# Gram matrices stored by row, inverse inputs in 2 loads, one PSUM bank moved from the chain's output to the passes

## The chip, the core and the metric

The kernel runs on one core of a Trainium2 chip. What is measured is the device time of one execution, in microseconds (us); smaller is better. The core has a matrix engine (PE), three engines for elementwise work (DVE, ACT, POOL), and an engine SP that here does nothing but issue nearly all DMAs. Every engine works through its own list of instructions in a fixed order, so an instruction that waits holds up all that stand behind it on the same engine. PE's results go to PSUM, which this kernel uses as 8 banks of 128 partitions x 512 fp32.

## What is computed

One block of a hybrid network, for 2048 tokens of width 1024, in fp32. A normalised input is multiplied by one wide weight matrix; two branches use the result, and their gated outputs are added to the input:

```
h = rms_norm(x, norm_g) * (1 + scale) + shift
p = h @ w_in                       # 1024 x 5960, in parts: pr pk pv pwd pad z_a q ckv z_b qi ki wi g_a g_b
y_a = rwkv7_branch(pr, pk, pv, pwd, pad, ...)      # a recurrence over all tokens, 8 heads of 64
    # per token: state = state*w + (state a) b^T + v k^T ; y = state r
y_b = dsa_branch(q, ckv, qi, ki, wi, ...)          # attention over the 256 best keys of each query
merged = sigmoid(g_a) * ((y_a * silu(z_a)) @ w_pa) + sigmoid(g_b) * ((y_b * silu(z_b)) @ w_pb)
out = rms_norm(x + gate * (merged @ w_o), final_g)
```

Only the recurrence (`rwkv7_branch`) is touched by the change.

## The kernel before

Each fp32 operand of a large product is split into a high and a low part, and a product is the sum of three matmuls (high x high, high x low, low x high). Tokens are cut into 4 blocks of 512. The stages, in the time of the trace: the start up to 130 us, the index GEMM up to 400, the selection of keys up to 840; from there to 1740 the recurrence, with the rest of the wide GEMM laid between its steps; the first branch's product (`branch_a`) from 1699 to 1816, attention up to 2240, the finish up to 2534.

The wide GEMM is done in units (`unit`, L251): 48 matmuls `g`, of 24 k-steps and two halves of 256 columns, into one of two banks named `g`, which ACT or DVE then empties into an SBUF tile `eo` (`evacuate`) for a store. Its last jobs make the gates: columns `g`, stored to `gg` in DRAM.

The recurrence of one block of 512 tokens has three parts.

- `rwkv_pass` (L612 to L720), per pair of heads: loads rows of the wide product (`pk`, `pr`, `pv`), makes decays and keys, and the Gram matrices of 64-token chunks: `pg` at L703, masked by DVE into `gt` (L705) and stored to `gmd` in DRAM (L706). Its PSUM tiles are all named `pg` and come from the pool `rwpa` (L544).
- `rwkv_inv` (L722 to L747): loads `ln` from `gmd` (L730), 64 problems (8 chunks x 8 heads) for each diagonal 32 x 32 sub-block, and inverts them on DVE by 31 steps of forward substitution (`prd` L740, `tm` L742), then stores the inverses.
- `rwkv_chain` (L749 to L821): 8 chunks one after the other, each of which needs the state `H` of the chunk before. A chunk loads its matrices (`gmc` at L762 among them), then PE does `zu`, `pp`, `zu`, `hp` (L777 to L801), and DVE forms the new state from `hp` (L806). Every four chunks `chain_norm` and `chain_out` normalise the outputs `y`; PE transposes them into a tile `co` (L854), DVE scales them (L855), and a store sends them to `ya`. The tiles `zu`, `pp`, `hp` and `co` are one PSUM bank each.

The 8 banks of this stage are thus 2 for `g`, 4 for the chain and 2 for `pg`; after the last pass `heads` (L862) takes the two of `pg` for its own products `p`.

The order on each engine is set ahead of time by a scheduler: each part of the program has a priority (`self.band`, L1246 to L1286: pass 50000, chain 50000 to 55000, GEMM 60000 to 70000, `branch_a` 75000), and the scheduler places instructions by a simulated timeline in which a tile's buffer must be free. A larger number is later work that fills in. DMAs stand in SP's list in the same way; each one also waits for the DMA eight places before it in its lane of eight semaphores.

Where the GEMM ends, `branch_a` starts. It first splits its weights `w_pa`, in four chunks of 128 x 1024, into `w_pah` and `w_pal` (L1018 to L1020), in SBUF space that the GEMM's pools leave, and so only when the last `gg` store has landed; then its `br` matmuls (L1111) run, whose inputs `uh` and `ul` come from `z` and `y` (L1042 to L1051), and `y` from `ya`.

Of the kernel before, what the change touches and what calls it, by code (L numbers as in the profile page):

```python
# [24 lines left out]
FT = mybir.dt.float32  # L25
# [6 lines left out]
PSUM = bass.MemoryType.PSUM  # L32
# [5 lines left out]
NTB = S // TB  # L38
# [13 lines left out]
class Block:  # L52
# [479 lines left out]
    def rwkv_open(self, ctx):  # L532
        nc, x = self.nc, self.x
        V, A, G, DMA = nc.vector, nc.scalar, nc.gpsimd, nc.sync
        R = self.R = {}
        c1 = R["c1"] = self.pool("rwc", 1, side="right", ctx=ctx)
        R["ch"] = self.pool("rwch", 2, side="right", ctx=ctx)
        R["pctx"], R["qctx"], R["ictx"] = ExitStack(), ExitStack(), ExitStack()
        R["iv"] = self.pool("rwi", 1, side="right", ctx=R["ictx"])
        R["ld"] = self.pool("rwl", 2, side="right", ctx=R["pctx"])  # L540
        R["wk"] = self.pool("rww", 1, side="right", ctx=R["pctx"])
        R["st"] = self.pool("rws", 2, side="right", ctx=R["pctx"])
        R["pc"] = self.pool("rwpc", 1, PSUM, ctx=R["qctx"])
        R["ps"] = self.pool("rwpa", 2, PSUM, ctx=R["pctx"])  # L544

        def cols(n):
            R[n] = self.cols(c1, x[n], "c_" + n, 4)

        for n in ("w0", "a0", "k_k", "k_a", "r_k", "lnx_g", "lnx_b"):
            cols(n)  # L550
        for n, src in (("w0h", "w0"), ("a0h", "a0"), ("kah", "k_a")):
            R[n] = c1.tile([128, 4], FT, name=n)
            V.tensor_scalar(R[n], R[src], 0.5, None, op0=OP.mult)
        R["kai"] = c1.tile([128, 4], FT, name="kai")
        V.tensor_scalar(R["kai"], R["k_a"], -0.5, 1.0, op0=OP.mult, op1=OP.add)

        wa2 = R["ld"].tile([128, 512], FT, name="pk")
        DMA.dma_start(wa2[0:64], x["w2"])
        DMA.dma_start(wa2[64:128], x["a2"])
        w2, a2, l2 = (c1.tile([128, 512], FR, name=n) for n in ("w2s", "a2s", "wa2l"))  # L560
        R["w2"], R["a2"], R["l2"] = w2, a2, l2
        A.copy(w2[0:64], wa2[0:64])
        A.copy(w2[64:128], wa2[0:64])
        A.copy(a2[0:64], wa2[64:128])
        A.copy(a2[64:128], wa2[64:128])
        V.tensor_tensor(l2[0:64], wa2[0:64], w2[0:64].bitcast(FT), op=OP.subtract)
        V.tensor_tensor(l2[64:128], wa2[64:128], a2[64:128].bitcast(FT), op=OP.subtract)
        raw = R["ld"].tile([128, 512], FT, name="pk")
        R["oneht"] = c1.tile([40, 4, 128], FR, name="oneht")
        G.memset(raw[0:40], 0.0)  # L570
        DMA.dma_start(raw[0:8].rearrange("p (a b) -> p a b", a=4), x["k_oneht"])
        DMA.dma_start(raw[32:40].rearrange("p (a b) -> p a b", a=4), x["k_oneht"])
        A.copy(R["oneht"].rearrange("p a b -> p (a b)"), raw[0:40])
        R["oneh"] = c1.tile([128, 4, 8], FR, name="oneh")
        R["blk"] = c1.tile([128, 128], FR, name="blk")
        raw = R["ld"].tile([128, 512], FT, name="pk")
        DMA.dma_start(raw[:, 0:32].rearrange("p (a b) -> p a b", a=4), x["k_oneh"])
        DMA.dma_start(raw[:, 128:256], x["k_blk"])
        A.copy(R["oneh"].rearrange("p a b -> p (a b)"), raw[:, 0:32])
        A.copy(R["blk"], raw[:, 128:256])  # L580
        R["nr"] = c1.tile([40, 512], FR, name="nrs")
        G.memset(R["nr"].bitcast(FT), 0.0)
        scm = R["scm"] = c1.tile([128, 512], BF, name="scm")
        G.memset(scm, 1.0)
        G.memset(scm.rearrange("p (c t) -> p c t", t=64)[:, :, 0:1], 0.0)
        R["k_gm"] = c1.tile([128, 128], FT, name="k_gm")
        DMA.dma_start(R["k_gm"], x["k_gm"])
        R["eps"] = c1.tile([128, 1], FT, name="gneps")
        G.memset(R["eps"], 64e-5)
        R["H"] = []  # L590
        for i in range(2):
            h = c1.tile([128, 4, 128], FT, name=f"H{i}")
            G.memset(h, 0.0)
            R["H"].append(h)
        R["n"], R["late"] = 0, []
        d = self.d
        R["gm"] = [d.tile([8, 128, 8, 128], FT, name=f"gmd{i}") for i in range(NTB)]
        R["ar"] = [d.tile([8, 128, 4, 128], FT, name=f"ard{i}") for i in range(NTB)]
        R["bk"] = [d.tile([8, 128, 512], FT, name=f"bkd{i}") for i in range(NTB)]
        R["vt"] = [d.tile([512, 512], FT, name=f"vtd{i}") for i in range(NTB)]  # L600
        R["bo"] = [d.tile([512, 512], FT, name=f"bod{i}") for i in range(NTB)]
        R["ti"] = [d.tile([64, 32, 32], FT, name=f"tid{i}") for i in range(NTB)]
        R["tt"] = [d.tile([2, 64, 32, 32], FT, name=f"ttd{i}") for i in range(NTB)]
# [8 lines left out]
    def rwkv_pass(self, tb):  # L612
        nc, R = self.nc, self.R
        V, A, T, G, DMA = nc.vector, nc.scalar, nc.tensor, nc.gpsimd, nc.sync
        ld, wk, st, ps = R["ld"], R["wk"], R["st"], R["ps"]
# [28 lines left out]
        for p in range(4):  # L644
# [53 lines left out]
            for c0 in (0, 4):  # L698
                for hh in range(2):
                    r_ = slice(hh * 64, hh * 64 + 64)  # L700
                    pt = pg((128, 4, 128))
                    for j in range(4):
                        T.matmul(pt[:, j], bk[r_, c0 + j, :], ar[r_, c0 + j, :], start=True, stop=True)  # L703
                    gt = st.tile([128, 4, 128], FT, name="gt", bufs=4)
                    V.tensor_tensor(gt, pt, gm4, op=OP.mult)  # L705
                    DMA.dma_start(R["gm"][tb][c0:c0 + 4, :, 2 * p + hh, :].rearrange("c q t -> q c t"), gt)  # L706
            G.tensor_tensor(bk, bk, e65[:, :, 64:65].to_broadcast([128, 8, 128]), op=OP.mult)
            for c0 in (0, 4):
                pt = pg((128, 4, 128))
# [5 lines left out]
            pt = pg((128, 4, 128))  # L715
# [6 lines left out]
    def rwkv_inv(self, tb):  # L722

        nc, R = self.nc, self.R
        V, G, DMA = nc.vector, nc.gpsimd, nc.sync
        st = R["iv"]
        ln = st.tile([128, 32, 32], FT, name="ln", bufs=1)
        for b in range(2):
            for c in range(8):
                DMA.dma_start(ln[b * 64 + c * 8:b * 64 + c * 8 + 8],  # L730
                              R["gm"][tb][c, b * 32:b * 32 + 32, :, b * 32:b * 32 + 32].rearrange("s h t -> h s t"))
        tm = st.tile([128, 32, 32], FT, name="tm", bufs=1)
        G.memset(tm, 0.0)
        G.memset(tm.rearrange("p a b -> p (a b)")[:, ::33], 1.0)
        prd = st.tile([128, 1024], FT, name="prd", bufs=1)

        for s in range(31):
            r, n = 31 - s, s + 1
            v = prd[:, :r * n].rearrange("p (t j) -> p t j", t=r)
            V.tensor_tensor(v, ln[:, s, n:][:, :, None].to_broadcast([128, r, n]),  # L740
                            tm[:, s, 0:n][:, None, :].to_broadcast([128, r, n]), op=OP.mult)
            V.tensor_tensor(tm[:, n:, 0:n], tm[:, n:, 0:n], v, op=OP.add)  # L742
        tt = ln
        V.tensor_copy(tt.rearrange("p s t -> p t s"), tm)
        DMA.dma_start(R["ti"][tb], tm[0:64])
        DMA.dma_start(R["tt"][tb][0], tt[0:64])
        DMA.dma_start(R["tt"][tb][1], tt[64:128])  # L747

    def rwkv_chain(self, tb):  # L749
# [8 lines left out]
        for c in range(8):  # L758
            arc = ch.tile([128, 4, 128], FT, name="arc")
            DMA.dma_start(arc, R["ar"][tb][c])  # L760
            gmc = ch.tile([128, 8, 128], FT, name="gmc")
            DMA.dma_start(gmc, R["gm"][tb][c])  # L762
            bkc = ch.tile([128, 512], FT, name="bkc")
            DMA.dma_start(bkc, R["bk"][tb][c])
            uv = ch.tile([128, 512], FT, name="uv")
# [70 lines left out]
    def chain_out(self, tb, half, yt, yvar):  # L836
# [10 lines left out]
        def out(p):  # L847
            bo = ch.tile([128, 2, 256], FT, name="bo")
            DMA.dma_start(bo, self.rows(R["bo"][tb], p, t_))
            pt = pc.tile([128, 2, 256], FT, name="co")  # L850
            for k in range(2):
                f_ = slice((p + k) * 128, (p + k) * 128 + 128)
                for i in range(2):
                    T.transpose(pt[:, k, i * 128:(i + 1) * 128], yt[i].rearrange("q h v -> q (h v)")[:, f_], self.ident)  # L854
                V.scalar_tensor_tensor(bo[:, k], pt[:, k], R["lnx_g"][:, p + k:p + k + 1], bo[:, k],  # L855
                                       op0=OP.mult, op1=OP.add)
            DMA.dma_start(self.rows(self.YA[tb], p, t_), bo)
# [4 lines left out]
    def heads(self, ctx):  # L862
# [1 line left out]
        V, A, T, DMA = nc.vector, nc.scalar, nc.tensor, nc.sync  # L864
        k1 = self.pool("kv1", 1, side="right", ctx=ctx)
        w = self.pool("kvw", 3, side="right", ctx=ctx)
        ps = self.pool("kvp", 2, PSUM, ctx=ctx)
        U = []
        for n in ("w_uk", "w_uv"):
            r = w.tile([128, 512], FR, name="hi").bitcast(FT)  # L870
# [506 lines left out]
```

## Time and profile before

| | us |
|---|---|
| median of 3 runs | 2543.67 (2540.09 to 2544.42) |
| the profiled execution | 2535.82 |
| its span in the trace | 2534.0 |
| PE busy in it | 2414.3 (95%) |
| DVE, ACT, POOL busy | 1615.2, 1235.3, 804.8 |

The profiled execution took 1.8 us more than its span, and lies 7.85 us under the median. PE is busy nearly all the time, so a change is worth what it takes from PE's idle time or adds to it, and where that idle time lies is seen in a table of stretches. Granted clock 1.00 means that PE ran at 2.4 GHz, its upper level.

### The profile page before, as it was taken

The numbers are of one execution on the slowest core, as the hardware profiler recorded it, in microseconds if no ns is written. First come the engines' busy times: TensorE is split into PE (matmuls) and PEld (weight loads), VectorE is DVE, ScalarE is ACT, GpSimd is POOL, SyncE is SP. The second block draws the span as 40 slices with busy tenths as digits, with TensorE's granted clock in tenths as the row PEclk, the third lists the DMA queues.
The fourth block names the chain that finished last, engine by engine and source line by source line (L and its number), as shares of the span: only waits on it lengthen the run. The fifth ranks groups of instructions, "written<-read, shape, count | busy, mean of one in ns | idle before, by whom it ended". The sixth has DMA issues, their size and how long they took to land.

```text
span 2534.0 us, 44949 instructions
## 1 busy us (share of the span) xinstructions
PE 2414.3 (95%) x16776; PEld 2134.6 (84%) x16776; DVE 1615.2 (64%) x3381; ACT 1235.3 (49%) x2024; POOL 804.8 (32%) x694
## 2 busy tenths in 40 slices
PE   4899999999999999999999999999889999989998
PEld 3687878888888998889888989989779999988887
DVE  6614778776877556654936757344478888876443
ACT  4414646555544424334434333352478888865332
POOL 2411111111121333233333332131255555544332
PEclk9999999999999999999999999999999999999999
DMA  7754223423336556777677769978753343155442
GB/s 248 280 152 125 89 83 92 125 96 96 104 98 217 147 164 193 191 203 225 194 206 212 214 188 276 298 240 250 232 166 87 91 118 99 29 182 192 142 150 71
DMA packets 423496, 415.67 MB, mean 164 GB/s; under 512 B 80010, under 2 KB 339890, under 8 KB 418404
## 3 DMA queue, kind: packets, MB, share of 16 engines
q1 hardware_dynamic: 422692, 404.33, 53.1%
q0 software_dynamic: 576, 8.39, 0.8%
q8 instruction: 132, 2.16, 0.4%
q14 instruction: 96, 0.79, 0.1%
HBM read 254.04 MB, written 160.15 MB: 163 GB/s over the span
## 4 chain that ended last, share of the span: by engine, by line
PE 49%; DMA 7%; DVE 5%; issue 3%; ACT 2%; SPq 2%; POOL 2%; POOLq 0%; ACTq 0%; DVEq 0%
PE g L251 16%; PE fo L1196 6%; PE yv L993 4%; PE br L1111 4%; PE pt L976 3%; PE pg L703 2%; PE lg L959 2%; PE lg L960 2%; DMA xt<-in_w_pb_dram 1%; PE pp L808 1%; PE pp L791 1%; PE zu L797 1%; PE hp L801 1%; PE pp L788 1%; DVE prd L740 1%
## 5 line engine op out<-in xcount | busy, mean ns | idle before, releaser
L251 PE MATMUL g<-hh,whi 128*128 128x256 f32 (+1 forms) x2176 | 718.9, 330 | 8.8 <-DVE eo L265 4.7
L251 PE MATMUL g<-hl,whi 128*128 128x256 f32 (+1 forms) x2176 | 715.3, 329 | 2.9 <-POOL hl L169 2.9
L251 PE MATMUL g<-hh,wlo 128*128 128x256 f32 (+1 forms) x2176 | 714.9, 329 | 1.4 <-POOL wlo L237 1.4
L237 POOL TENSOR_TENSOR wlo<-wraw,whi 128x1024 fp32r<-128x1024 f32 (+1 forms) x89 | 225.1, 2529 | 748.3 <-ACT whi L236 695.0
L251 PEld LDWEIGHTS g<-hh,whi 128*128 128x128 f32 x2176 | 416.0, 191 | 54.7 <-issue 6.5
L251 PEld LDWEIGHTS g<-hl,whi 128*128 128x128 f32 x2176 | 416.2, 191 | 43.4 <-issue 4.1
L251 PEld LDWEIGHTS g<-hh,wlo 128*128 128x128 f32 x2176 | 416.0, 191 | 41.7 <-issue 4.3
L431 DVE SCALAR_TENSOR_TENSOR sc<-re,wi,sc 128x1024 f32<-128x1024 f32 (+7 forms) x154 | 170.7, 1108 | 56.7 <-ACT re L425 50.8
L425 ACT ACTIVATE re<-ixs 128x1024 f32<-128x1024 f32 (+7 forms) x176 | 140.4, 816 | 135.5 <-PE ixs L423 78.7
L236 ACT CAST whi<-wraw 128x1024 fp32r<-128x1024 f32 (+1 forms) x89 | 92.8, 1043 | 174.2 <-PE g L251 132.3
L976 PE MATMUL pt<-ident,lt 128*128 128x128 f32 x1088 | 168.1, 275 | 7.0 <-ACT tp L982 4.3
L966 ACT ACTIVATE lt<-lt,nm 128x128 f32<-128x128 f32 (+15 forms) x128 | 154.8, 1212 | 15.3 <-DVE nm L965 15.2
L987 DVE TENSOR_TENSOR pl<-pt,ph 128x512 fp32r<-128x512 f32 (+1 forms) x216 | 139.0, 657 | 31.6 <-ACT ph L986 30.7
L423 PE MATMUL ixs<-kim,st 128*128 128x512 f32 (+3 forms) x608 | 150.2, 373 | 8.3 <-ACT re L425 4.8
L962 DVE CUSTOM_DVE_ANT_0 lt<-lg,mask 128x512 f32<-128x512 f32 (+3 forms) x256 | 147.4, 589 | 16.5 <-PE lg L960 9.0
L993 PE MATMUL yv<-ph,vp 128*128 128x256 f32 (+1 forms) x576 | 152.1, 285 | 5.7 <-ACT ph L986 5.6
L993 PE MATMUL yv<-pl,vp 128*128 128x256 f32 x576 | 153.0, 301 | 2.0 <-POOL pl L984 1.8
L959 PE MATMUL lg<-m,sq 128*128 128x256 f32 (+3 forms) x384 | 136.6, 365 | 5.9 <-DMA mask<-mask 4.1
L423 PEld LDWEIGHTS ixs<-kim,st 128*128 128x128 f32 x608 | 113.1, 190 | 34.5 <-ACT re L425 6.9
L976 PEld LDWEIGHTS pt<-ident,lt 128*128 128x128 f32 x1088 | 125.7, 141 | 16.9 <-ACT tp L982 5.3
L986 ACT CAST ph<-pt 128x512 fp32r<-128x512 f32 (+1 forms) x216 | 116.4, 564 | 20.8 <-PE pt L976 14.3
L960 PE MATMUL lg<-m,sq 128*128 128x256 f32 (+3 forms) x384 | 126.2, 336 | 0.0
(343 smaller groups left out, 5106.6 us busy)
## 6 DMA issues: line engine op xcount, KB each, us to landing
wraw<-in_w_in_dram SPq DMA_DIRECT2D x88, 512.0 KB
gg<-eo SPq DMA_DIRECT2D x64, 256.0 KB
gmd<-gt SPq DMA_DIRECT2D x64, 256.0 KB
gmc<-gmd SPq DMA_DIRECT2D x32, 512.0 KB
g<-gg SPq DMA_DIRECT2D x64, 256.0 KB
m<-ks SPq DMA_DIRECT2D x32, 512.0 KB
pj<-eo SPq DMA_DIRECT2D x52, 256.0 KB
x<-in_ada_w_dram SPq DMA_DIRECT2D x24, 512.0 KB
```

Of the source, the lines that this page charges most:

```text
L237: nc.gpsimd.tensor_tensor(lo[:, :, :n], raw[:, :, :n], hi[:, :, :n].bitcast(FT), op=OP.subtract)
L251: T.matmul(p[:, s], a[:, k], b[:, k, s], start=n == 0, stop=n == 3 * KD - 1)
L423: T.matmul(p[:, a:b], st[:, h], M[i][:, k0 + a:k0 + b], start=i == 0, stop=i == 1)
L425: A.activation(r[:, :kn], p[:, :kn], AF.Relu)
L431: V.scalar_tensor_tensor(o, r[:, :kn], wi, o, op0=OP.mult, op1=OP.add)
L959: T.matmul(p[:, :kn], sq[:, qb * 128:(qb + 1) * 128], m1[:, k0:k1_], start=True, stop=False)
L960: T.matmul(p[:, :kn], sq[:, qb * 128:(qb + 1) * 128], m2[:, k0:k1_], start=False, stop=True)
L962: V.tensor_tensor_reduce(lt[:, k0:k1_], p[:, :kn], mk, 1.0, -3.0e38, OP.subtract, OP.max, cm[:, i:i + 1])
L966: ex = A.activation(lt[:, :n], lt[:, :n], AF.Exp, bias=nm, accum_out=lsum[:, qb, h:h + 1])
L976: T.transpose(p[:, o:o + 128], L[i][:, kt * 128:(kt + 1) * 128], self.ident)
L993: T.matmul(yv[:, qs], vp[:, kt, :], b[:, o:o + nn], start=kt == 0 and i == 0, stop=kt == last and i == 1, skip_group_check=True)
L1196: T.matmul(p, a[:, k, q], b[:, k, s], start=n == 0, stop=n == 23)
```

## The change

There are four edits. The Gram matrices of a block lie in DRAM as [128 rows, 8 chunks, 8 heads, 128] where they lay as [8 chunks, 128 rows, 8 heads, 128]; the store (L706) and the chain's load (L762) follow. With that layout chunk and head can be read as one dimension of stride 128, so `ln` is loaded by 2 DMAs of 64 partitions (256 KB) where it was 16 of 8 partitions (32 KB); the bytes and their pieces of 32 floats are the same. The transposed outputs are put into a tile named `hp`, which shares the one bank of the state products, and no longer into `co`. And the bank that this frees is given to the pools of the passes (`rwpa`) and of the heads (`kvp`), 3 where it was 2.

```diff
-        R["ps"] = self.pool("rwpa", 2, PSUM, ctx=R["pctx"])
+        R["ps"] = self.pool("rwpa", 3, PSUM, ctx=R["pctx"])
-        R["gm"] = [d.tile([8, 128, 8, 128], FT, name=f"gmd{i}") for i in range(NTB)]
+        R["gm"] = [d.tile([128, 8, 8, 128], FT, name=f"gmd{i}") for i in range(NTB)]
-                    DMA.dma_start(R["gm"][tb][c0:c0 + 4, :, 2 * p + hh, :].rearrange("c q t -> q c t"), gt)
+                    DMA.dma_start(R["gm"][tb][:, c0:c0 + 4, 2 * p + hh, :], gt)
-            for c in range(8):
-                DMA.dma_start(ln[b * 64 + c * 8:b * 64 + c * 8 + 8],
-                              R["gm"][tb][c, b * 32:b * 32 + 32, :, b * 32:b * 32 + 32].rearrange("s h t -> h s t"))
+            b_ = slice(b * 32, b * 32 + 32)
+            DMA.dma_start(ln[b * 64:b * 64 + 64], R["gm"][tb][b_, :, :, b_].rearrange("s c h t -> (c h) s t"))
-            DMA.dma_start(gmc, R["gm"][tb][c])
+            DMA.dma_start(gmc, R["gm"][tb][:, c])
-            pt = pc.tile([128, 2, 256], FT, name="co")
+            pt = pc.tile([128, 2, 256], FT, name="hp")
-        ps = self.pool("kvp", 2, PSUM, ctx=ctx)
+        ps = self.pool("kvp", 3, PSUM, ctx=ctx)
```

The file is one line shorter from L730 on: what is L854 or L1111 before is L853 or L1110 after. The scheduler's order moves with the buffers. Three places are shown.

SP's list around the `ln` loads of the first block, before (`bkd` and `vtd` are the pass's other stores, `lat` and `qs` stores of the GEMM, `pk` the first load of the second block's pass):

```order
L706 DMA gmd_8668<-gt 128x4x128 x2
L230 DMA wraw<-in_w_in_dram 128x8x128
L762 DMA gmc<-gmd_8668 128x1024 x2
L730 DMA ln<-gmd_8668 8x32x32 x8
L714 DMA bkd_8676<-gt 128x4x128
L75 DMA lat_76<-eo 128x512
...
L720 DMA vtd_8680<-gt 128x4x128
L730 DMA ln<-gmd_8668 8x32x32 x6
L75 DMA qs<-eo 64x512 x4
...
L730 DMA ln<-gmd_8668 8x32x32 x2
L633 DMA pk<-pj_69 128x512
```

and now:

```order
L706 DMA gmd_8668<-gt 128x4x128 x2
L340 DMA pj_71<-eo 128x512
L230 DMA wraw<-in_w_in_dram 128x8x128
L714 DMA bkd_8676<-gt 128x4x128
L730 DMA ln<-gmd_8668 64x32x32
L714 DMA bkd_8676<-gt 128x4x128
L720 DMA vtd_8680<-gt 128x4x128
L730 DMA ln<-gmd_8668 64x32x32
L648 DMA pv<-pj_69 128x512
L763 DMA bkc<-bkd_8676 128x512 x2
L633 DMA pk<-pj_69 128x512
```

The last `ln` load stands 7 places behind the last `gmd` store where it stood 37 places behind it; the `pk` load follows a few places later in both.

PE's list where the GEMM's last unit ends, before (`zu`, `pp`, `hp` are chunks 30 and 31 of the chain, `br` is the first of `branch_a`):

```order
L251 MATMUL g<-hh,wlo 128x256
L782 MATMUL zu<-ttc,t1c 32x32 x8
L788 MATMUL pp<-H_8664,arc 128x128 x4
L791 MATMUL pp<-uv,gmc 64x64 x8
L797 MATMUL zu<-xx,ttc 64x64 x8
L1111 MATMUL br<-uh_18972,w_pah 128x256
...
L1111 MATMUL br<-ul_18973,w_pah 128x256
L801 MATMUL hp<-uv,bkc 128x128 x4
L808 MATMUL pp<-uv,gmc 64x64 x8
L777 MATMUL zu<-t1c,gmc 32x32 x8
L1111 MATMUL br<-uh_18972,w_pal 128x256 x2
```

and now:

```order
L251 MATMUL g<-hh,whi 128x256
L251 MATMUL g<-hl,whi 128x256
L251 MATMUL g<-hh,wlo 128x256
L1110 MATMUL br<-uh_18916,w_pah 128x256
L1110 MATMUL br<-ul_18917,w_pah 128x256
L1110 MATMUL br<-uh_18916,w_pah 128x256
L1110 MATMUL br<-ul_18917,w_pah 128x256
```

No chain matmul stands between the last `g` and the `br` any more. The chain's last instruction on PE is now this one, with 189 matmuls `g` between it and the first `br`:

```order
L251 MATMUL g<-hl,whi 128x256
L251 MATMUL g<-hh,wlo 128x256
L853 MATMUL hp<-ident,y 128x128 x2
L251 MATMUL g<-hh,whi 128x256
L251 MATMUL g<-hl,whi 128x256
```

The chain has moved forward past the end of the GEMM, which therefore ends later on PE than it did, with less left to lay behind it.

## Rows read from the trace of the kernel before

**Rows 1.** The page, busy us and share of the span by engine

```profile
PE 2414.3 (95%) x16776; PEld 2134.6 (84%) x16776; DVE 1615.2 (64%) x3381; ACT 1235.3 (49%) x2024; POOL 804.8 (32%) x694
```

**Rows 2.** Stretches: us, busy PE, PEld, DVE, ACT, POOL, clock, DMA, GB/s

```profile
840.00:1000.00 160.00, 156.31 (x1196) 145.75 (x1196) 81.36 (x123) 62.29 (x92) 54.32 (x46) 0.99 0.56 165
1000.00:1100.00 100.00, 91.01 (x676) 83.05 (x675) 71.62 (x114) 35.12 (x53) 32.24 (x21) 0.97 0.70 194
1540.00:1740.00 200.00, 196.30 (x1928) 183.31 (x1929) 107.67 (x196) 82.71 (x141) 43.57 (x44) 0.99 0.86 265
1740.00:1860.00 120.00, 100.68 (x744) 95.41 (x744) 54.00 (x147) 48.97 (x90) 31.34 (x36) 0.94 0.80 247
```

**Rows 3.** Waits from 985 to 1100: us, times, longest

```profile
ACT pk L634 <- DMA pk<-pj: 8.0, 3, 6.8
DVE prd L740 <- DMA pk<-pj: 5.7, 1, 5.7
PE g L251 <- DVE eo L265: 4.7, 3, 2.7
PE pg L636 <- ACT kk L608: 1.4, 1, 1.4
```

**Rows 4.** SP from 1007 to 1035: start, us, DMA

```profile
1011.44 6.57 SPq L730 DMA_DIRECT2D ln<-gmd  x8
1024.26 3.54 SPq L730 DMA_DIRECT2D ln<-gmd  x6
1032.22 0.88 SPq L730 DMA_DIRECT2D ln<-gmd  x2
1033.15 0.35 SPq L633 DMA_DIRECT2D pk<-pj  x1
```

**Rows 5.** The tile ln: its loads, and DVE's idle time before it

```profile
L740 DVE TENSOR_TENSOR prd<-ln,tm x124: 181/374/2554, 1037.9 to 1577.4; 128x31 f32<-128x31 f32 x8, 128x60 f32<-128x60 f32 x8, 128x87 f32<-128x87 f32 x8, 128x112 f32<-128x112 f32 x8
L730 SPq DMA_DIRECT2D ln<-gmd x64: 264/413/2757, 1011.4 to 1535.1; - x64
  DMA ln<-gmd: 5.6, 1
```

**Rows 6.** The end of the GEMM by engine: start, us, instruction, idle before

```profile
1693.39 0.28 PE L251 MATMUL g<-hh,wlo 128*128 128x256 f32 x1
1694.31 0.32 SPq L349 DMA_DIRECT2D gg<-eo  x1
1697.91 1.99 ACT L1019 CAST w_pah<-xt 128x1024 fp32r<-128x1024 f32 x2 [0.26 <-DMA gg<-eo]
1699.98 3.22 POOL L1020 TENSOR_TENSOR w_pal<-xt,w_pah 128x1024 fp32r<-128x1024 f32 x1
1704.23 0.42 SPq L1018 DMA_DIRECT2D xt<-in_w_pa_dram  x1
1708.13 1.04 ACT L1019 CAST w_pah<-xt 128x1024 fp32r<-128x1024 f32 x1 [1.53 <-DMA xt<-in_w_pa_dram]
1709.68 2.36 POOL L1020 TENSOR_TENSOR w_pal<-xt,w_pah 128x1024 fp32r<-128x1024 f32 x1
1712.10 0.39 PE L1111 MATMUL br<-uh,w_pal 128*128 128x256 f32 x1 [0.37 <-POOL w_pal L1020]
```

**Rows 7.** Two stretches, as in group 2

```profile
1693.40:1712.10 18.70, 15.59 (x178) 13.94 (x176) 9.97 (x11) 9.58 (x15) 9.90 (x6) 0.91 0.53 160
1712.10:1815.70 103.60, 95.18 (x778) 93.20 (x778) 41.22 (x67) 31.13 (x51) 12.86 (x10) 0.98 0.77 240
```

**Rows 8.** The same stretch, `br` alone: us, busy PE, PEld, DVE, clock

```profile
1693.40:1712.10 18.70, 4.34 (x23) 3.43 (x23) 0.00 (x0) 0.91 0.53 160
```

**Rows 9.** Waits from 1693 to 1816, PE's from 1712.1

```profile
POOL y L1043 <- DMA y<-ya: 46.2, 7, 13.1
PE br L1111 <- DVE g L1116: 4.6, 2, 3.9
```

**Rows 10.** The tile co: first and last start us of its reader

```profile
L855 DVE SCALAR_TENSOR_TENSOR bo<-co,c_lnx_g,bo x32: 451/480/485, 1183.3 to 1738.3; 128x256 f32<-128x256 f32 x32
```

## The prediction

> **What bounds the kernel now.** I read the engines' busy times first. PE is busy 2414.3 us of a span of 2534.0 [rows 1], and the change leaves its matmuls as they are, so it can only take from PE's 120 us of idle time or add to them. The second view is the table of stretches, read for PE's busy time against the length of each [rows 2]. The recurrence touches three of them: 840 to 1000 has 3.7 us of idle, 1000 to 1100 (where the first block's inverse and the second block's pass run) 9.0, and 1540 to 1740 3.7. The stretch from 1740 to 1860 has 19.3, most of them in the passage to attention, which is not touched. Third, the waits of the 9.0 us: PE's largest is for DVE emptying a `g` bank, 4.7 in all, and PE waits 1.4 for `kk`, made from the `pk` load whose landing held ACT for 6.8 [rows 3]. Last, the end of the GEMM by engine. The last `g` matmul starts at 1693.39; the `w_pa` split waits until the last `gg` store has landed and then runs through two casts, a split on POOL, a load, a cast and a split, so that `br` flows freely only from 1712.10 [rows 6]. In these 18.7 us PE is busy 15.59 [rows 7], of which 23 `br` take 4.34 at a granted clock of 0.91 [rows 8] and the last two chunks of the chain the other 11.25.
>
> **The 16 loads made 2.** There are 64 loads before, 413 ns of SP at the median [rows 5], and 8 after. For the first block SP spent 6.57 + 3.54 + 0.88 = 10.99 us on them, and put the `pk` load behind the last, at 1033.15 [rows 4]. Eight issues in 6.57 us are 0.82 each, so two are 1.6 and SP gains about 9 us. That is no gain of PE by itself: DVE's first `prd` waited 5.7 us (the row names the `pk` load, which SP issued just behind the last `ln`) [rows 3], in another block 5.6 for `ln` itself [rows 5], and PE had `g` matmuls meanwhile. In the changed order the last `ln` load still stands right behind the pass's last stores, with few DVE instructions left to lay before `prd`; I expect a DVE wait of 4 to 6 us again. What becomes earlier is `pk` and so the second block's pass. Bounds for the landing of one large load: from the end of the last issue, 1033.10 [rows 4], to the `prd` at 1037.9 [rows 5] are 4.8 us, which is the low end; the high end is all 10.99 us of the sixteen issues spent on pieces, 15.8. I take 5.5, nearest to the measured waits.
>
> **Layout.** The Gram stores keep their pieces of 512 bytes, and a chunk's load keeps 4 KB per partition, at a larger stride. I take 0; the bounds are −1 and +3 us, since the chain's loads come a chunk ahead of use.
>
> **The third bank of the passes.** It removes waits of a matmul for a `pg` that is still being read. Of the 9.0 us of idle from 1000 to 1100 I let half go, for the earlier `pk`, the `pg` bank and the changed places of DVE's `eo`: −4.5, with bounds of 0 and −9. In the other stretches of passes and chain PE is idle for 0.6 us at most outside 1693 to 1712 (3.7 less 18.70 − 15.59 = 3.1), so nothing more is to be had there.
>
> **The shared bank.** A transposed output must now wait until DVE has added the last state product, and the next state product until DVE has read the output, 0.48 us for each half [rows 10]. In the changed order the output transposes stand some 10 us of PE's matmuls ahead of the next `hp`. I take 0: PE fills a late chunk with `g`. The cover is the 189 `g` matmuls behind the chain's last PE instruction, 23 us at 95.18 / 778 = 0.122 us each [rows 7]. If it were gone, 16 output tiles of two halves would delay the chain by 16 x 2 x 0.48 = 15 us, which still fits. Bounds 0 and +4.
>
> **The end of the GEMM.** Here the change costs. By the order the chain is through before the GEMM ends, and nothing but `br` stands behind the last `g`. The path to the free flow stays: copy and store 0.92 us from the start of the last `g`, landing 3.60 (1694.31 to 1697.91), two casts and their gap 2.07, POOL's split 3.22, the load to the cast 3.90, the cast 1.04, POOL 2.36 [rows 6]: 17.1 us. The 1.0 us of SP and 0.5 of POOL that lay between for the chain fall away. In that time PE can do 22 `br`, 22 x 0.122 = 2.7 us, and loses 14.4. Before, it lost 18.70 − 23 x 0.122 − 11.25 = 4.6 there. The difference is +9.8; the chain's 11.25 us ran at a mean clock of 0.91 and would be up to 9%, 1.0 us, shorter among `g`, of which I take 0.6, so +9.2. The clock may be low for some `br` matmuls after a longer pause; the stretch before already had 0.91, and I add nothing. Bounds: +5, if the store and the load land 2 us sooner each with the queue emptier, and +12.
>
> The Trainium skill bears on this path. On its page "DMA: Bandwidth & Descriptors", section on the anatomy of one DMA, it fits a transfer's time as 2.0 us plus the bytes at 436 GB/s, for GpSimd's path. An estimate by that page for the 256 KB store is 2.6 us and for the 512 KB load 3.2, where the rows show 3.60 and 3.90; the sum would be 1.7 us smaller by it. These DMAs are SP's and the rows are theirs, so I stay with the rows.
>
> **The first branch.** It takes 103.6 us with PE busy 95.18 [rows 7]. POOL waits 46.2 us for `y<-ya`, and PE 4.6 for DVE's `g` [rows 9]. The chain's last output is read at 1738.3 [rows 10], in the middle of this stretch; after the change it has gone before it. −1, with bounds of −4 and +3. Between the chain's blocks the order changes too: +1, bounds 0 and +4.
>
> **Sum.** −4.5 + 9.2 − 1 + 1 = +4.7 us, of which the two large terms are about equally unsure. The profiled execution would go from 2535.8 to 2540.5. It lay 7.85 us under the median of the three runs, and I let the same difference stand: 2543.67 + 4.7 = 2548.4, given as 2548.
>
> **Rivals.** *SP's relief pays in full.* All 9.0 us of idle go, the end of the GEMM costs only its low bound of +5, and the first branch gains its 4: −8, 2535.7. For it speaks that ACT's 6.8 us wait was for a load that stood behind the last `ln` load; against it, that in the new order `pk` still stands behind `ln`, and that the `br` cannot flow before four weight chunks are split.
>
> *The large loads land late.* This is the slow case. DVE stands at `prd`, and behind it in its fixed list stand the `eo` that empty `g`. PE has two `g` banks, and a unit is 48 x 0.122 = 5.9 us. DVE's 5.7 us wait is just about covered, so from about 6 us on each further microsecond costs PE one, in all 4 blocks. With a wait half way up to the bound, (4.8 + 15.8) / 2 = 10.3, it is 4 x 4.4 = +18: 2566. For it: the same number of pieces is now in one transfer whose last piece must land before DVE may start, where part of the sixteen used to land early. Against it: the wait of before was as long with only two small loads outstanding, so it is mostly not made of pieces. The Trainium skill, on the same page in its section on why a DMA increments its semaphore by 16, says that a DMA uses the largest number of engines up to 16 that divides its slowest dimensions; by that a load of 8 partitions ran on 8 engines and one of 64 runs on 16, which speaks against this rival. No row here shows how many engines a load used.
>
> *Nothing reaches PE.* The layout and loads are hidden, and the gap at the GEMM's end is as long as before since it was set by the weight chunks either way: about 0, 2543.7. Against it speaks that 11.25 us of chain work lay in that gap.
>
> **Chances.** A measurement of this kernel can tell about 0.2%, 5.1 us, from no change. My forecast has 0.55: 0.31 of it under 2548.8 and 0.24 above, since 4.7 lies close to the bound. The full relief has 0.27, of which 0.22 faster and 0.05 same; the late loads 0.10, slower; nothing 0.08, of which 0.07 same and 0.01 slower. Together: faster 0.22, same 0.43, slower 0.35. The likeliest case by itself runs from 2541 to 2555. The range for 8 in 10 goes down to 2534, just below the full relief, and up to 2560, part of the way to the late loads.
>
> **What would show it.** The gap at the GEMM's end: from the last `g` matmul to the free flow of `br` 16 to 18 us, with PE busy 3 to 5 of them and no `zu`, `pp` or `hp` among them. PE's idle time in the 100 us that hold the first inverse: 9.0 before, 4 to 5 after. DVE's idle time before the first `prd` of each block: 4 to 6 us; over 8 would be the late loads. Reads of the transposed outputs that end before the last `g`. I am wrong if the chain still runs beside `br`, if the gap is under 10 us, or if the front gains more than the end loses.

## The result, and the profile after

The changed kernel took 2552.43 us (median of 13 runs, 2546.43 to 2562.88), the kernel before 2541.24 (13 runs, 2532.96 to 2547.13). The ratio is 1.0053, with a 95% interval of 1.0041 to 1.0066: slower by some 13 us, where the forecast was +4.7. Below, one execution of the kernel with the outputs in `hp` alone (2958.69 us at a granted clock of 0.749) is left out of its ratio.

The first line of the page, to be set against [rows 1]:

```profile
PE 2429.3 (95%) x16776; PEld 2144.1 (84%) x16776; DVE 1612.3 (63%) x3381; ACT 1230.0 (48%) x2022; POOL 804.2 (31%) x694
```

PE is busy 15 us longer with the same matmuls, so more than idle time has changed. The table of stretches below follows the program and not the clock on the wall: from the first Gram product to the last one; on to the last `g` matmul of the wide GEMM; from there to the first `br` that flows freely; and on to the end of the first branch. The columns are those of [rows 2] (busy PE, PEld, DVE, ACT, POOL with their counts, then granted clock, DMA share, GB/s). The kernel before, whose last two stretches are those of [rows 7] but for a tenth of a microsecond or two:

```profile
898.10:1522.20 624.10, 612.60 (x5503) 555.01 (x5503) 371.78 (x624) 227.63 (x366) 213.58 (x184) 0.99 0.69 200
1522.20:1693.60 171.40, 170.81 (x1699) 158.34 (x1697) 86.83 (x171) 66.92 (x117) 34.54 (x40) 1.00 0.92 282
1693.60:1712.10 18.50, 15.38 (x176) 13.87 (x175) 9.77 (x11) 9.58 (x15) 9.90 (x6) 0.91 0.52 157
```

The changed kernel:

```profile
905.80:1470.00 564.20, 551.21 (x4922) 492.74 (x4922) 360.37 (x613) 209.75 (x342) 199.47 (x176) 0.97 0.73 209
1470.00:1722.40 252.40, 252.40 (x2463) 236.67 (x2461) 104.19 (x204) 88.02 (x153) 53.17 (x53) 1.00 0.75 230
1722.40:1737.30 14.90, 6.99 (x24) 5.16 (x23) 2.45 (x2) 4.67 (x5) 4.75 (x2) 0.59 0.28 88
1737.30:1846.40 109.10, 97.71 (x746) 95.56 (x746) 35.25 (x53) 28.40 (x47) 12.83 (x10) 0.93 0.70 219
```

The two long stretches together grew from 795.5 to 816.6 us; they hold 183 more matmuls, the last two chunks of the chain and their outputs. The passage to `br` shrank from 18.5 to 14.9, but PE is busy 7 of them instead of 15.4, at a granted clock of 0.59. The branch grew from 103.6 to 109.1. A second profile of each kernel gave the same picture (918.4 us for the four stretches of before, 936.7 for the changed one, against 917.6 and 940.6), so the surplus of some 20 us in this part is no accident of one execution. It is more than the 13 us of the timed runs: both profiles of before are of executions under its median, both of the changed kernel of executions above its median.

The passage itself. PE:

```profile
1722.19 0.28 PE L251 MATMUL g<-hh,wlo 128*128 128x256 f32 x1
1726.35 0.58 PE L1110 MATMUL br<-uh,w_pah 128*128 128x256 f32 x1 [3.88 <-ACT w_pah L1018]
...
1728.21 0.42 PE L1110 MATMUL br<-ul,w_pah 128*128 128x256 f32 x1
1728.42 0.41 PE L1110 MATMUL br<-uh,w_pal 128*128 128x256 f32 x1
...
1737.28 0.58 PE L1110 MATMUL br<-uh,w_pal 128*128 128x256 f32 x1 [1.21 <-POOL w_pal L1019]
```

and what it waits for, on ACT, SP and POOL (answers to [rows 6]):

```profile
1723.16 0.32 SPq L349 DMA_DIRECT2D gg<-eo  x1
1725.25 1.99 ACT L1018 CAST w_pah<-xt 128x1024 fp32r<-128x1024 f32 x2 [2.12 <-DMA gg<-eo]
1727.38 2.40 POOL L1019 TENSOR_TENSOR w_pal<-xt,w_pah 128x1024 fp32r<-128x1024 f32 x1 [24.67 <-ACT w_pah L1018]
1727.58 2.55 SPq L1017 DMA_DIRECT2D xt<-in_w_pa_dram  x2
1733.76 1.05 ACT L1018 CAST w_pah<-xt 128x1024 fp32r<-128x1024 f32 x1 [1.53 <-DMA xt<-in_w_pa_dram]
1734.88 2.35 POOL L1019 TENSOR_TENSOR w_pal<-xt,w_pah 128x1024 fp32r<-128x1024 f32 x1 [5.10 <-ACT w_pah L1018]
```

After the last `g` PE has nothing to do for 3.9 us, until the `gg` store has landed and the first `w_pah` is cast; then it does a few `br` and waits for each chunk. The free flow comes at 1737.28, 15.1 us after the start of the last `g`. The `br` in a row start 0.21 us apart, where it is 0.12 at the upper clock.

### The profile page after: what moved, and what is told of

Its sections match the earlier page's. It is cut to its first block, busy times and chain, and to the rows that moved or that the text cites. A ratio compares the mean times of both kernels' runs of the same rounds, so it can differ in the third digit from the quotient of the medians.

```text
span 2561.1 us, 44925 instructions
## 1 busy us (share of the span) xinstructions
PE 2429.3 (95%) x16776; PEld 2144.1 (84%) x16776; DVE 1612.3 (63%) x3381; ACT 1230.0 (48%) x2022; POOL 804.2 (31%) x694
## 4 chain that ended last, share of the span: by engine, by line
PE 49%; DMA 7%; DVE 6%; issue 3%; ACT 2%; POOL 2%; SPq 1%; POOLq 0%; ACTq 0%; DVEq 0%
PE g L251 15%; PE fo L1195 5%; PE yv L992 4%; PE br L1110 4%; PE pt L975 3%; PE lg L958 2%; PE lg L959 2%; PE pg L703 2%; PE zu L796 1%; PE pp L790 1%; PE pp L807 1%; PE pp L787 1%; PE hp L800 1%; DMA gg<-g 1%; PE zu L781 1%
## 5 line engine op out<-in xcount | busy, mean ns | idle before, releaser
L965 ACT ACTIVATE lt<-lt,nm 128x128 f32<-128x128 f32 (+15 forms) x128 | 154.8, 1212 | 13.8 <-DVE nm L964 13.7
L961 DVE CUSTOM_DVE_ANT_0 lt<-lg,mask 128x512 f32<-128x512 f32 (+3 forms) x256 | 147.6, 589 | 15.2 <-PE lg L959 7.3
```

The costliest lines, as they stand in the source:

```text
L961: V.tensor_tensor_reduce(lt[:, k0:k1_], p[:, :kn], mk, 1.0, -3.0e38, OP.subtract, OP.max, cm[:, i:i + 1])
L965: ex = A.activation(lt[:, :n], lt[:, :n], AF.Exp, bias=nm, accum_out=lsum[:, qb, h:h + 1])
```

## Experiments

Each kernel was timed against the kernel before on the same chip, in 12 or 13 executions, in 6 for the PSUM edits and the early split, and in 4 for the filled passes and the bank given to `g`. The ratios, and the granted clock as a mean over the timed executions (before: 0.984 to 0.985; the changed kernel without one execution at 0.930, which took 2557.39 us and so was among the others):

| kernel | ratio to before | 95% interval | clock |
|---|---|---|---|
| layout alone, 16 loads | 1.0002 | 0.9989 to 1.0016 | 0.984 |
| layout and 2 loads | 1.0035 | 1.0018 to 1.0051 | 0.983 |
| outputs in `hp` alone | 1.0062 | 1.0039 to 1.0085 | 0.983 |
| and 3 banks for the passes | 1.0101 | 1.0084 to 1.0117 | 0.977 |
| and 3 banks for the heads | 1.0082 | 1.0055 to 1.0109 | 0.977 |
| all: the changed kernel | 1.0053 | 1.0041 to 1.0066 | 0.979 |
| all, last two chunks held back | 1.0020 | 1.0005 to 1.0036 | 0.981 |
| all, gap filled | 1.0044 | 1.0029 to 1.0059 | 0.982 |
| all, `w_pa` split early | 1.0067 | 1.0045 to 1.0089 | 0.979 |
| all, passes filled | 1.0106 | 1.0084 to 1.0128 | 0.981 |
| outputs in `hp`, bank given to `g` | 1.0139 | 1.0118 to 1.0161 | 0.977 |

**The layout and the two loads, without the PSUM edits** (of the change, the lines on `gm` and `ln`).

> Only the layout and the two ln loads; PSUM as before. Theory (the loss comes from the third PSUM bank of the passes, which packs passes and chain together, lowers the granted clock there and empties the end of the GEMM): the chain still runs beside br, so the gap at the GEMM's end stays near 5 us of lost PE time, PE's slow-clock time stays near before's, and the time is within 5 us of before (2537 to 2546). Rival (the large loads land late and hold DVE): this kernel carries the loss, about 2553, with DVE idle over 8 us before the first prd of each block.

Slower by 0.35%, between the two theories. The loads are not late: they land in 3.1 to 6.0 us, and DVE's four waits for `ln` before a first `prd` are 12.8 us in all, none over 4.6. So the loss comes near the size of the rival, without its mechanism. The passage is a milder form of that of the changed kernel (PE idles 5.6 us in it, before 3.1), and the branch is as long as there:

```profile
1700.60:1716.30 15.70, 10.14 (x103) 8.43 (x101) 7.07 (x11) 8.26 (x11) 6.08 (x3) 0.93 0.41 120
1716.30:1825.80 109.50, 99.70 (x754) 97.46 (x754) 38.01 (x59) 28.08 (x47) 12.86 (x10) 0.92 0.73 225
```

In the passage stand 103 matmuls where before has 176, and the chain's last `hp` starts 6.7 us after the last `g`, where it is 22 before; the branch then takes 109.5 us at a clock of 0.92.

**The layout alone**, with the 16 loads (the list of every engine stays in the order of before, and only the addresses differ; the lines on `gmd` and `gmc` are those of the change and left out here):

```diff
+            b_ = slice(b * 32, b * 32 + 32)
             for c in range(8):
-                DMA.dma_start(ln[b * 64 + c * 8:b * 64 + c * 8 + 8],
-                              R["gm"][tb][c, b * 32:b * 32 + 32, :, b * 32:b * 32 + 32].rearrange("s h t -> h s t"))
+                DMA.dma_start(ln[b * 64 + c * 8:b * 64 + c * 8 + 8], R["gm"][tb][b_, c, :, b_].rearrange("s h t -> h s t"))
```

> Only the layout of the Gram matrices; ln still in 16 loads of 8 partitions, so that every engine's list is in the order of before. If the loss of the kernel with layout and two loads (0.35%) comes from the order that the scheduler made of it: as before, within 4 us (2538 to 2547), granted clock 0.983 to 0.985. If the larger stride of the rows costs the loads: that loss is here, 2550 to 2554, with landings later and PE or DVE waiting for gmc or ln.

The same as before: the larger stride costs nothing that the interval can tell. What the kernel with two loads loses comes with the two loads, and since these are not late, I put it down to the order that the scheduler made for them.

**The PSUM edits by themselves**, in three steps: the outputs in `hp`; with that 3 banks for the passes; with that 3 for the heads.

> The transposed outputs in hp, and nothing else; one bank of PSUM is left unused. Theory (sharing costs nothing, its price in the prediction was 0): within 4 us of before, clock 0.983 to 0.985. Rival (outputs and state products hold each other up): 8 us slower or more, with the chain's hp or the outputs' transposes waiting for DVE and the chain's end later.

> Outputs in hp and the third bank for the passes alone; heads keep 2, loads and layout as before. Theory of the passes' bank: it carries the loss of the PSUM edits, 10 to 21 us slower than before, mean granted clock 0.976 to 0.979, slow-clock time of 20 us or more in the passes of blocks 1 to 3. If the heads' bank is the cause: at most 3 us slower, clock as before.

> Only the PSUM edits (outputs in hp, 3 banks for passes and heads); 16 loads and layout as before. Theory of the PSUM bank: the whole loss is here, 2549 to 2556, with the chain through before the last g matmul, 13 to 15 us of lost PE time at the GEMM's end and granted clock under 1.00 in stretches of passes and chain. Rival of the loads: no loss, 2541.

The sharing alone costs 0.62%, the rival's side, though its waits are small. Waits of PE from 890 to 1835 us (us, times, longest), of which only the second is for the shared bank, and its first two stretches:

```profile
PE hp L801 <- DVE uv L798: 3.1, 4, 1.6
PE hp L854 <- DVE bo L855: 1.5, 2, 1.3
```

```profile
896.90:1526.50 629.60, 615.27 (x5416) 555.76 (x5416) 366.88 (x617) 222.08 (x358) 208.07 (x183) 0.98 0.68 195
1526.50:1711.20 184.70, 183.50 (x1822) 168.46 (x1820) 90.60 (x178) 71.82 (x128) 37.12 (x41) 1.00 0.91 275
```

These two stretches are 814.3 us, 18.8 longer than in the first profile of before, with only 36 more matmuls. PE's idle time there is 15.5 us where two profiles of before have 12.1 and 14.0. Summed over pieces of 1 us, PE ran 23.9 us of them at the lower clock, in the two profiles of before 6.8 and 3.4.

The third bank of the passes adds to that (1.0062 to 1.0101, where the intervals just touch) and takes the clock down to 0.977. It is also what empties the end of the GEMM. With the sharing alone PE is still busy 14.6 of the 18.7 us of the passage; with the third bank for the passes, and the old loads and layout, the passage is that of the changed kernel:

```profile
1724.10:1738.90 14.80, 7.13 (x25) 5.18 (x23) 2.45 (x2) 4.67 (x5) 4.74 (x2) 0.58 0.28 89
```

The heads' bank changes nothing that the intervals can tell. The parts do not add up: the two loads lose 9 us by themselves, and beside the PSUM edits they seem to win 7 (1.0082 to 1.0053, where the intervals just overlap). Each edit makes the scheduler lay out the whole stretch anew.

**The last two chunks held back.** In the changed kernel, the last block's chunks 6 and 7 get a priority between the GEMM's and the branch's:

```diff
         for c in range(8):
+            if tb == NTB - 1 and c == 6:
+                self.band(74000)
```

> The changed kernel with the chain's last two chunks given a later priority, so that their matmuls stand between br again, as before the change; nothing is added. If the gap at the GEMM's end is worth what the prediction gave it (+9.2): PE's idle time in the gap falls from 8 to under 4 us, the slow-clock time in it from 13 to under 7, and the kernel is 7 to 12 us faster than the changed one, 1.001 to 1.003 of before. If the gap is a symptom and the passes carry the loss: within 4 us of the changed kernel, 1.004 to 1.006.

```profile
903.70:1463.00 559.30, 546.38 (x4923) 487.63 (x4922) 360.33 (x613) 209.78 (x342) 197.98 (x176) 0.98 0.73 211
1463.00:1699.50 236.50, 236.50 (x2259) 222.84 (x2257) 95.57 (x185) 81.89 (x142) 51.65 (x51) 1.00 0.77 239
1699.50:1719.10 19.60, 18.04 (x195) 16.29 (x194) 5.01 (x7) 7.77 (x12) 6.81 (x4) 0.83 0.27 82
1719.10:1822.30 103.20, 95.21 (x780) 93.20 (x778) 41.83 (x67) 30.98 (x51) 12.86 (x10) 0.98 0.77 241
```

The chain's matmuls stand between the `br` again, PE is busy 18.0 of 19.6 us, the branch is back at 103.2, and the whole is 918.6 us as before the change. The time goes from 1.0053 to 1.0020, 8.4 of the 13.5 us, and the two intervals do not overlap. The idle time came down as the theory of the gap said, and the time at the lower clock in the passage from 12.3 us to 6.8. Not all of the 8.4 us need be the gap: the branch came back with it, and the two long stretches were laid out anew (795.8 us with 203 matmuls less than the 816.6 us of the changed kernel).

**The gap filled with work that nobody reads**, in the changed kernel:

```diff
+        if "g" in kinds and tbs[0] == 2:
+            p = self.gps.tile([128, TB], FT, name="g")
+            for n in range(24):
+                T.matmul(p[:, :256], wts[0][0][:, n % 8], self.HT[3][0][:, n % 8, :256], start=True, stop=True)
...
+            pd = ps.tile([128, 2, FB], FT, name="br", bufs=self.pbufs)
+            for n in range(64):
+                T.matmul(pd[:, 0], hi[:, 0, :128], hi[:, 0, 128:384], start=True, stop=True)
```

> The changed kernel with 88 matmuls added in the gap at the GEMM's end, whose results nobody reads: 24 right behind the last g, 64 on the first w_pa chunk, 10.7 us of PE work. If the lowered clock after the gap is a cost of the gap: the slow-clock time there (17 us in the changed kernel) shrinks to under 7, and the kernel is 1 to 4 us faster than the changed one in spite of the added work, about 2550. If the gap is a wait alone: the same as the changed kernel, 2552. If PE was not free there: up to 10 us slower, 2562.

The passage and the branch:

```profile
1715.40:1730.80 15.40, 13.52 (x111) 13.11 (x109) 2.45 (x2) 4.68 (x5) 4.80 (x2) 1.00 0.27 86
1730.80:1833.20 102.40, 93.64 (x746) 91.84 (x746) 35.48 (x53) 28.28 (x47) 12.88 (x10) 0.97 0.73 233
```

88 matmuls more cost nothing: the passage is as long as it was, its clock is 1.00, and the branch takes 102.4 us where it took 109.1 and, in the second profile of the changed kernel, 106.9. Not all of these 4 to 7 us are the clock that the gap left low. In both profiles of the changed kernel PE ran 17.1 us at the lower clock from the gap on, of which 5 us lie in the branch; with a `br` every 0.21 us instead of every 0.12 they cost some 2 us. The kernel with the filled passes (below) has the same gap with the same 17.1 us, and its branch took 104.6. The rest is PE's idle time and falls of the clock later in the branch, which differ from one profile to the next. In the timed runs some 2 us remain, within the intervals.

**The `w_pa` split moved ahead** of the GEMM's last part, into the SBUF that the heads leave:

```diff
+        self.split_weights(self.WA, self.pool("ba1", 1, side="right", ctx=bctx),
+                           self.pool("bax", 2, side="right", ctx=bctx), (("w_pa", 4),), ...)
         self.gemm_half((2, 3), ("z", "g"))
```

> The changed kernel with the w_pa loads and splits moved ahead of the last part of the GEMM, into SBUF that the heads leave, so that br needs no chunk that comes after the last gg store. Theory of the gap: from the last g to the free flow of br 1 to 4 us instead of 15.7, and 10 to 15 us faster than the changed kernel: 2538 to 2543. If the loss is all in the passes' slow clock: only the idle that before had there too, about 4 us, goes, 2548.

A miss. The gap is not gone, and its reason is another. The largest wait of PE from 1690 to 1830 (us, times, longest):

```profile
PE br L1110 <- DMA g<-gg: 10.6, 1, 10.6
```

In the changed kernel the loads of the branch's own tiles `z`, `y` and `g` begin at 1604.7; here the first of them is issued at 1710.34, behind the last `gg` store of 1708.15. I read this as `w_pa` having taken their space: something has to wait for the SBUF of the GEMM, and moving one tenant ahead puts another behind.

**Matmuls added to the passes**, in the changed kernel, one in front of each group of Gram products of blocks 2 and 3:

```diff
+                    if tb >= 2:
+                        T.matmul(pt.rearrange("p a b -> p (a b)"), R["blk"], R["w2"], start=True, stop=True)
```

> The changed kernel with one 128x512 matmul added ahead of each Gram product group of the passes of blocks 2 and 3, whose result the Gram products overwrite: 32 matmuls, about 7 us of PE work. If the falls of the clock in these passes come of what PE does there (many small matmuls, few g): the slow-clock time in passes 1 to 3, 31 us in the changed kernel, falls by 10 or more, and the time is the same as the changed kernel's, within 4 us. If the falls have nothing to do with it: slow-clock time as it was, and 5 to 9 us slower than the changed kernel, 1.008 to 1.009 of before.

```profile
898.70:1468.20 569.50, 557.38 (x4962) 493.85 (x4961) 355.11 (x616) 208.55 (x340) 199.11 (x178) 0.99 0.72 207
1468.20:1721.10 252.90, 252.50 (x2456) 236.40 (x2454) 103.52 (x200) 89.72 (x155) 53.40 (x50) 1.00 0.75 230
1736.30:1840.90 104.60, 94.16 (x746) 92.14 (x746) 34.90 (x53) 28.29 (x47) 12.84 (x10) 0.96 0.74 228
```

The time at the lower clock in the passes falls to 13.7 us, where two profiles of the changed kernel have 30.7 and 27.3, so the first expectation held for the clock. It failed for the time: the two stretches are 6 to 8 us longer, about the work that was added, and the kernel is 0.5% slower than the changed one. One profile does not tell whether the clock stayed up for the added matmuls or for the order that the scheduler made with them, and what the clock of the passes is worth is not shown.

**The freed bank given to the GEMM**: every third unit of the second half takes a `g` from a pool of one bank, beside the outputs in `hp`.

> Outputs in hp, and the freed bank given to the wide GEMM (every third unit of the second half uses a third g bank) instead of the passes; 16 loads and old layout. If the passes' bank is what loses: faster than the kernel with the shared output alone (1.006 of before), since PE no longer waits for a g bank to be emptied (4.7 us before), 0.998 to 1.003. If any change of the order loses: 1.005 or more.

The slowest of all, and so no better use of the bank. Two further profiles, of before and of the changed kernel:

> The kernel before once more, for a second profile of it: 2538 to 2548 us, granted clock 0.982 to 0.986. In its first profile the clock was low for 58 us in all; here 60 to 85, since that execution was one of the fastest. Its place in passes 1 to 3 and at the GEMM's end should still be under 12 us, where the changed kernel has 44.

> The changed kernel once more, for a second profile: its first was of the slowest of its 13 executions. 2547 to 2557 us. From the first Gram product to the end of the first branch 934 to 941 us (before 917 and 918 in two profiles), with the granted clock low for 40 us or more in that span (before 14 and 21), of which 12 or more at the GEMM's end. If these were accidents of the first profile: under 930 and under 25.

2539.52 us at a clock of 0.986, and 2555.87 at 0.979. Both came out as expected; the clock of the second was low for 51 us in these stretches, 12 of them in the gap. Its stretches, as above:

```profile
902.90:1465.20 562.30, 548.60 (x4923) 489.63 (x4922) 359.96 (x613) 209.88 (x342) 198.96 (x176) 0.98 0.73 210
1465.20:1717.60 252.40, 252.40 (x2463) 236.63 (x2461) 104.21 (x204) 87.88 (x153) 53.14 (x53) 1.00 0.75 230
1717.60:1732.70 15.10, 6.95 (x24) 5.15 (x23) 2.45 (x2) 4.67 (x5) 4.74 (x2) 0.61 0.28 87
1732.70:1839.60 106.90, 96.26 (x746) 94.20 (x746) 35.41 (x54) 28.50 (x47) 12.82 (x10) 0.94 0.71 223
```

No kernel tried here beats the one before. The best of them that keeps the change is the one with the chunks held back.

## Why the prediction came out as it did

The direction was right, the size was not: some +13 us where +4.7 was forecast. The time lies inside the range because the end of the GEMM came out near its price; that a gain which did not come and a cost that was not in the sum did not carry it further is luck.

*What bounds it.* Right: PE, and the places where it idles.

*The 16 loads made 2.* Right but for the size of DVE's wait. The answer to [rows 5]:

```profile
L730 SPq DMA_DIRECT2D ln<-gmd x8: 592/624/3225, 1012.0 to 1475.6; - x8
  DMA ln<-gmd: 5.0, 3
DMA to landing us min/median/max: 4.7/5.2/5.5
```

8 issues, a landing of 5.2 us at the median where 5.5 was taken between 4.8 and 15.8, and DVE idle for 5.0 us in all three waits together, where 4 to 6 were expected in each block. The late loads of the rival did not happen. The edit as a whole has a price of its own that the sum did not have (1.0035), since the order goes with it.

*Layout*, 0: right, 1.0002.

*The third bank*, −4.5: this step failed. The stretch from 1000 to 1100 was to lose half of its 9.0 us of idle; PE is now busy 90.64 of 100 us there, 9.4 idle. The answer to [rows 3]:

```profile
PE pg L658 <- ACT gt L719: 3.0, 1, 3.0
PE zu L776 <- DMA t1c<-tid: 2.0, 1, 2.0
PE pg L636 <- ACT kk L608: 1.5, 1, 1.5
PE g L251 <- DVE eo L265: 0.7, 1, 0.7
```

The waits on which the 4.5 us rested did shrink (`g` for DVE from 4.7 to 0.7 us), and others took their places: `pg` for ACT's copy, `zu` for a load of the chain. Over both long stretches PE idles 13.0 and 13.7 us in two profiles of the changed kernel and 12.1 and 14.0 in those of before, so nothing was won. In full: these stretches grew by 21.1 and 19.2 us in the two profiles, against the first of before. The work moved into them cost 15.2 us where it stood before (11.25 in the gap, and 3.9 of `hp`, `pp` and output transposes in the branch). So the front lost 4 to 6 us and did not gain 4.5. The kernel with the chunks held back, with the passes in the new order and within 20 matmuls the same work, needs 795.8 us for them, as before, though PE ran 20.5 us of them at the lower clock. Whether the bank wins something there that the clock takes back stays open.

What I had not put into the sum is the clock. It was half for 31 and 27 us of these stretches in two profiles of the changed kernel, and for 7 and 3 in those of before. Stretches of 2 us around one such fall, in the changed kernel (columns as above):

```profile
1404.00:1406.00 2.00, 2.00 (x29) 1.48 (x25) 1.73 (x3) 0.00 (x0) 0.35 (x1) 1.00 1.16 300
1406.00:1408.00 2.00, 2.00 (x14) 1.75 (x14) 0.69 (x2) 0.36 (x1) 1.22 (x1) 0.89 0.90 271
1408.00:1410.00 2.00, 2.00 (x10) 1.78 (x9) 0.15 (x1) 0.00 (x0) 0.00 (x0) 0.50 1.13 343
1412.00:1414.00 2.00, 2.00 (x16) 1.88 (x16) 0.80 (x2) 0.00 (x0) 1.85 (x3) 0.50 0.43 131
1418.00:1420.00 2.00, 2.00 (x20) 2.00 (x19) 0.00 (x0) 0.43 (x1) 0.00 (x0) 1.00 0.03 8
```

PE is busy without a gap on both sides of it. What stands on PE from 1400 to 1408:

```profile
L703 PE MATMUL pg<-ar,bk 64*128 64x128 f32 x24 | 3.1, 289 | 0.0
L251 PE MATMUL g<-hh,wlo 128*128 128x256 f32 x10 | 3.1, 309 | 0.0
L781 PE MATMUL zu<-ttc,t1c 32*32 32x32 f32 x16 | 0.7, 192 | 0.0
```

24 small Gram products and 16 matmuls of 32 x 32 stand there between 30 `g` (one of their three lines is shown). The kernel before has such a stretch too, with 24 Gram products, 44 matmuls of the chain and 11 `g`, and its clock stayed up:

```profile
1312.00:1319.00 7.00, 7.00 (x79) 6.46 (x78) 2.87 (x6) 0.95 (x2) 1.53 (x3) 1.00 0.73 204
```

So what brings these falls about stays open. The Trainium skill, "TensorE: Matmul & The Clock Gate", part 1, gives the lower clock as the state after an idle stretch, with busy-ness as what raises it. Here the rows say busy and the clock falls, so a busy PE in a row is no proof against a fall.

*The shared bank*, 0: wrong by itself (1.0062). The wait that I had weighed is small, 1.5 us in all; what differs is the order around it and the time at the lower clock, and how much each costs is not shown. The outputs are read early enough, as foreseen ([rows 10]): the last one at 1699.8, before the last `g`:

```profile
L854 DVE SCALAR_TENSOR_TENSOR bo<-hp,c_lnx_g,bo x32: 471/484/485, 1202.6 to 1699.8; 128x256 f32<-128x256 f32 x32
```

*The end of the GEMM*, +9.2: right in its mechanism and near in size. The gap was 15.1 us where 17.1 was worked out (16 to 18 was given as the sign of it), and the chain is gone from it. PE is busy 7.0 us in it instead of 3 to 5, since its `br` run at a clock of 0.59; at the upper clock they are 2.7 us, so 12.4 are lost where 4.6 were: +7.8. Putting the two chunks back wins 8.4, with the clock behind the gap in it.

Of the 2.0 us that the gap is shorter, the store's landing gave 1.5 (2.1 us where [rows 6] had 3.6, at a DMA share of 0.28 where it was 0.52) and POOL's first split 0.8 (2.40 where it had 3.22); the load to the cast took as long as in the rows, 3.9 to 4.0. By the estimate from the Trainium skill's page "DMA: Bandwidth & Descriptors", anatomy of one DMA, the gap was to be 1.7 us shorter than from the rows. That the totals are close is luck: its 2.6 us for the store and 3.2 for the load are too long and too short, and POOL's share is not in it.

*The clock after the gap*, 0: failed, by a little. "I add nothing" should have been some +2: that is what 5 us at the lower clock cost in the branch, and what the timed runs with the gap filled show, if within their intervals.

*The first branch*, −1: it took 109.1 and 106.9 us where it had 103.6 and 104.3, though the chain's 3.9 us had gone. Some 2 us of this are the clock just told, and 2 to 5 are PE's idle time (11.4 and 10.6 us, before 8.4 and 6.6); the rest is not accounted for. With the gap filled it took 102.4, near the forecast.

Of the rivals, full relief and late loads are out. What stays open is the last 0.2%, the difference between the kernel with the chunks held back and the kernel before, which none of the four stretches shows; what the two loads lose when they stand alone; and why the sharing alone costs as much as all four edits together.

## What to carry to other kernels

A chain that runs late beside a throughput stage may be the filler of that stage's end: before making it earlier, look at what PE does in the next place where everything waits for memory to come free. In a program whose order a scheduler makes, an edit of buffers is an edit of the whole order, and its parts neither add up nor can be priced by the waits that they remove; keep one variant with the old order and the new data (here the layout alone) to tell the two apart. Price a pause of PE with the clock that follows it, here some 2 us behind a gap of 15.

## What was not expected of the hardware

Executions of one kernel differ with their granted clock: 0.001 less goes with about 2.1 us more over 12 timed executions of the changed kernel and with 1.4 to 2.5 over four sets of 7 to 23 of before; the execution at 0.930 does not follow this. The clock fell to half in stretches where PE was busy throughout. Loads of 256 KB in pieces of 128 bytes landed in 3.1 to 6.2 us in three profiles.
